# An issue order made in several passes, with a backward layout and estimates for partial and strided operations

## The chip, the cores and the metric

The kernel runs on one core of a Trainium2 chip. A core has five engines that work side by side, each through its own stream of instructions in the order of issue: TensorE (PE, with its weight loads shown apart as PEld), VectorE (DVE), ScalarE (ACT), GpSimd (POOL) and SyncE (SP), which here only issues DMAs. An instruction that waits for another engine holds up everything behind it on its own engine. The metric is the device time in microseconds (us) of one launch.

## What is computed

Two layers are applied to a prompt of 512 tokens and a sample of 256 tokens, with the same weights and 1024 channels: layer 0 is a bidirectional Mamba-2 mixer, layer 1 a bidirectional RWKV-7 mixer, each followed by a residual and a LayerNorm.

```python
alpha = (2.0 * DEPTH) ** 0.25            # DEPTH = 2
h = _mamba2_mixer(x, ...)                # layer 0
x = _layernorm(alpha * x + h, ln_g[0], ln_b[0])
h = _rwkv7_mixer(x, ...)                 # layer 1
x = _layernorm(alpha * x + h, ln_g[1], ln_b[1])
...
def step(s, inp):                        # RWKV-7, one token, once forwards and once backwards
    r_t, w_t, k_t, v_t, kk_t, a_t = inp
    sa = jnp.einsum('bhvk,bhk->bhv', s, -kk_t)
    s = (s * w_t[:, :, None, :] + sa[..., None] * (kk_t * a_t)[:, :, None, :]
         + v_t[..., None] * k_t[:, :, None, :])
    return s, jnp.einsum('bhvk,bhk->bhv', s, r_t)
...
y = (y - mu_y) * lax.rsqrt(var_y + R_GN_EPS) * ln_w + ln_b
out = (y + bonus) * g                    # then out @ w_out
```

All numbers are float32.

## The kernel before

**Arithmetic.** The 768 tokens of both sequences are handled together. A dense float32 product is three matmuls in a reduced float32 format: each operand is split into a high and a low part, and `mm3` (L140 to L142) adds high x high, high x low and low x high. Weights come in through `load_w`: a DMA (L121), a cast on ACT that makes the high part `whi` (L122), and a subtraction on DVE that makes the low part `wlo` (L123). The activations `xT` are loaded and split in the same manner (DMA L189, cast L135, subtraction L136).

**Stages.** First come the Mamba layer with its input projections, its chunked scan, its output projection and its LayerNorm. Then comes RWKV, in eight blocks `b` of 128 channels (two heads each). For a block, `rwkv_in` makes the projections r, k, v, g (dense matmuls, `pj`) and writes some of them to DRAM; the normalized key needs a row of norms that makes a trip through DRAM (`rows` L790, `rsd`, DMA `rb` L795) before DVE can form `k` (L796). `p1` works on six windows of 256 tokens: `p1_front` loads the block's streams again as `Wr` (DMA L853) and makes the decays (ACT L862 to L869); `p1_back` multiplies them on POOL into `G` (L888, L890) and takes matmuls of them (`ptd` L899). `rwkv_inverse` inverts the triangular matrices of all chunks: a long row of small DVE pairs (L949, L950), two transposes on DVE (L951, L953), and then the end of the inverse:

- PE multiplies the off-diagonal quarter (`pe`, L963) in two groups of 16 and 8 chunks,
- ACT writes each group back (L965, two instructions per group),
- ACT copies the diagonal quarters into `TD` (L968, L969; 32 partitions, a strided read; 16 chunks, "32x16x32", twice each, and 8 chunks, "32x8x32", twice each),
- PE multiplies again (`px`, L973), which needs all of L965, and L976 puts the result into `TD`.

The first `chain_step`s of the block need `px`; the copies of 8 chunks concern the sample's second half of chunks and are first read at step 4. `rwkv_final` normalizes the block's output `Y` per head: `rsqrt` on DVE by Newton steps (L102 to L107, `ngy`), a product on POOL (L1087), transposes on PE (`pf` L1091), ACT (L1097), POOL (L1100), DVE (L1101). In the program `p1(b+1)`, `rwkv_final(b)` and `rwkv_inverse(b+1)` follow the chain steps of block b. At the end stands the output projection with LayerNorm (L497, L512 to L526, `lnv` L522).

**The order.** The program text only lays out what is to be done. `arrange` (L1741) builds a `Program`: the graph of dependencies, and for each instruction an estimated duration (`estimate`, L1336). `schedule` (L1534) then is a list scheduler: it walks forward in an estimated time, and whenever an engine is free it takes the ready instruction with the best priority. The priority is the length of the longest path to the end (`tails`, L1516), in which every engine is taken to be free. A `Machine` (L1685) models what the scheduler believes of the engines: the clock of PE, modes of the PE array, DVE and POOL getting in each other's way, the DMA queue. For PE, four numbers (`Params`, L1245) decide when dense and small matmuls change places. The order that results is fixed for each engine; data waits come on top. One rule of `estimate` that the change touches (L1393): an ACT operation of N elements per partition is estimated at 51 + 0.8333 N ns, and 43 ns more without PSUM.

Of the kernel before, what the change touches and what calls it, by code (L numbers as in the profile page):

```python
# [58 lines left out]
class Trunk:  # L59
# [9 lines left out]
    def __init__(self, ctx, tc, d, y_p, y_s):  # L69
        self.ctx, self.tc, self.nc, self.d = ctx, tc, tc.nc, d  # L70
        self.out = (y_p, y_s)

        self.steps, self.gates, self.gate = {}, [], None
        self.cst = self.pool("cst", 1)
        self.bigx = ctx.enter_context(ExitStack())
        self.open_big(self.bigx, KB)
        self.pj = self.pool("pj", 1, PSUM, ctx=self.bigx, side="right")
        self.dr = self.pool("dr", 1, DRAM)
        self.ln_sm = self.pool("lnsm", 2)
        self.ident = self.cst.tile([P, P], F32, name="ident")  # L80
# [1155 lines left out]
NODE = "node"  # L1236
# [2 lines left out]
WARM = 2900  # L1239
SPAN = 3400  # L1240
TURN = 95.0
FULL = (128, 128)


class Params:  # L1245
    keep, pace, stay, spare = 4000.0, 1.6, 1000.0, 2.3


def size(ap, first=1):
    return math.prod(int(n) for _, n in ap.ap[first:])  # L1250
# [33 lines left out]
def space(t, name):  # L1284
    return str(t._space).endswith(name)


class Program:


    def __init__(self, nc, tc):
        self.ins = ins = list(nc.cur_bb.bb.instructions)
        n = len(ins)
        self.eng = [str(x.engine).split(".")[-1] for x in ins]
        self.pred = [set() for _ in ins]
        self.cost, self.dma, self.cols = [0.0] * n, [0.0] * n, [0.0] * n
        self.cells, self.kind = [()] * n, [1] * n
        self.mode, self.lock = [FULL] * n, [0.0] * n
        self.after, self.rationed = defaultdict(set), set()
        self.raw = set()  # L1300
        aps, self.acc = [], defaultdict(list)
        for i, x in enumerate(ins):
            io = [[a.bass_ap for a in l if getattr(a, "bass_ap", None) is not None] for l in (x.ins, x.outs)]
            aps.append(io)
            for b in io[0] + io[1]:
                if hasattr(b.tensor, "cap_key"):
                    self.acc[b.tensor.name].append(i)
            if io[0] or io[1]:
                self.estimate(i, x, *io)
        self.trace(nc, tc, aps)  # L1310
        self.classify()
# [24 lines left out]
    def estimate(self, i, x, src, dst):  # L1336
# [7 lines left out]
        if e == "PE":  # L1344
# [28 lines left out]
                self.kind[i] = 0  # L1373
            return
        N = max(size(a) for a in src + dst)
        ps = any(space(a.tensor, "PSUM") for a in src + dst if hasattr(a.tensor, "_space"))
        ptr = sum(1 for a in src if size(a) == 1 and N > 1)
        two = len(src) - ptr
        if e == "DVE":
            if op != "TensorScalarPtr":  # L1380
                c = (66 + N) / 0.96
                if op == "Reciprocal":
                    c = 70 + N * 6.4
            elif x.ins and two == 1 and not ps:
                c = 69 + N / 1.92 + 61 * ptr
            else:
                c = (66 + N) / 0.96 + 61 * ptr
            if getattr(x, "is_tensor_tensor_scan", False):
                c = 70 + 2.07 * N
            if not ps and N > 16:  # L1390
                self.lock[i] = c - 60
        elif e == "Activation":
            c = 51 + N * 0.8333 + (0 if ps else 43) + 93.5 * ptr + (93 if len(dst) > 1 else 0)  # L1393
        elif op == "Memset":
            c = 35 + 0.8333 * N
        elif op == "TensorScalarPtr":
            c = 130 + N * 0.83 + 90 * ptr
            self.lock[i] = c - 60
        elif two > 1:
            c = 160 + 1.6 * N if N < 200 else 190 + 1.75 * N  # L1400
            self.lock[i] = c - 60
        else:
            c = 130 + 0.9 * N
            self.lock[i] = c - 60
# [126 lines left out]
                    todo.append(j)  # L1531
        return tail

    def schedule(self, par=Params):  # L1534

        n, eng, pred, mode, kind = len(self.pred), self.eng, self.pred, self.mode, self.kind
        prio = [-v for v in self.tails()]  # L1540
        succ, asucc = [[] for _ in range(n)], defaultdict(list)
        for i, s in enumerate(pred):
            for j in s:
# [137 lines left out]
        del order[NODE]  # L1681
        return order


class Machine:  # L1685


    def __init__(self, p):
        self.p, self.free = p, defaultdict(float)
        self.mode, self.ring = FULL, 0.0  # L1690
        self.cell = [0.0] * 16
        self.work, self.held = defaultdict(float), {"DVE": 0.0, "Pool": 0.0}

    def run(self, i, t):

        p, e = self.p, self.p.eng[i]
        if e == NODE:
            return t
        if e == "PE":
            return self.matmul(i, t)  # L1700
        end = t + p.cost[i]
        if p.lock[i]:
            other = "Pool" if e == "DVE" else "DVE"
            end = max(end, self.held[other] + p.lock[i])
            self.held[e] = end
        self.free[e] = end
        if p.dma[i]:
            self.ring = max(self.ring, t + DMA_NS) + p.dma[i]
            end = self.ring
        return end  # L1710
# [73 lines left out]
```

## Time and profile before

| | |
|---|---|
| time before, median of 3 runs | 1726.08 us (1723.99, 1726.08, 1730.06) |
| the profiled execution's own time | 1718.15 us |
| its span | 1716.4 us |
| PE busy | 1546.6 us, 90% of the span, 15210 matmuls |
| DVE busy | 1362.4 us, 79%, 3041 instructions |
| ACT busy | 889.4 us, 52%, 1998 instructions |
| POOL busy | 758.4 us, 44%, 1026 instructions |
| mean granted clock of PE | 0.95 of full speed |

The profile comes from one execution. Its time is 1.75 us more than its span, and 7.93 us (0.46%) less than the median. "Busy" counts the time in which an engine executes; a busy PE may still run at a reduced clock, which the row PEclk gives in tenths of full speed. Rows of the timeline give the start, the duration, the engine and line, the output and inputs, and in brackets how long the engine was idle before and what ended this wait.

### The profile page before, as it was taken

Reading aid. Unit: us, or ns where it says so; the run is one execution under the profiler, and the core shown is the slowest. Engines: PE = TensorE matmul, PEld = TensorE weight load, DVE = VectorE, ACT = ScalarE, POOL = GpSimd, SP = SyncE. Lnnn points to the kernel's source line nnn. Section 1 sums busy time; section 2 is a strip of 40 time slices with the busy share of each in tenths; the row PEclk is TensorE's granted clock in tenths of the full one; section 3 lists DMA queues with packets and bytes.
Section 4 is the critical chain, followed back from the end, with each engine's and each line's share of the span. In section 5 each row is a group of like instructions: output and inputs, shape, how many; then the busy total and the mean of one; then the engine's idle time right before and its main releaser. Section 6 shows DMA issues by size and latency. Waiting matters only on the chain. (4 is left out here: it accounts for less than half of the span.)

```text
span 1716.4 us, 39466 instructions
## 1 busy us (share of the span) xinstructions
PE 1546.6 (90%) x15210; PEld 1302.3 (76%) x15210; DVE 1362.4 (79%) x3041; ACT 889.4 (52%) x1998; POOL 758.4 (44%) x1026
## 2 busy tenths in 40 slices
PE   7999999999999899998878989899898989878893
PEld 6887878888888799997667677677777767666783
DVE  5779988797897884678687878869797978969578
ACT  3344444545445442325556657485657657484432
POOL 1068356556565450021443626364554728274203
PEclk9999999999999899999988989889898989989996
DMA  5121211221211251603343243433434343444321
GB/s 162 38 62 32 69 56 38 62 81 56 69 44 56 66 169 60 201 38 114 111 133 116 83 125 86 123 102 109 132 99 130 88 119 91 126 144 123 116 62 74
DMA packets 150318, 161.42 MB, mean 94 GB/s; under 512 B 39633, under 2 KB 106929, under 8 KB 150129
## 3 DMA queue, kind: packets, MB, share of 16 engines
q1 hardware_dynamic: 150128, 158.89, 30.8%
q8 instruction: 120, 1.97, 0.5%
q14 instruction: 70, 0.57, 0.1%
HBM read 121.43 MB, written 40.55 MB: 94 GB/s over the span
## 5 line engine op out<-in xcount | busy, mean ns | idle before, releaser
L140 PE MATMUL pj<-xh,whi 128*128 128x256 f32 (+1 forms) x1056 | 385.0, 366 | 19.7 <-ACT whi L122 10.8
L142 PE MATMUL pj<-xh,wlo 128*128 128x256 f32 (+1 forms) x1056 | 381.5, 364 | 7.2 <-DVE wlo L123 7.2
L141 PE MATMUL pj<-xl,whi 128*128 128x256 f32 (+1 forms) x1056 | 381.7, 362 | 0.8 <-DVE xl L136 0.8
L140 PEld LDWEIGHTS pj<-xh,whi 128*128 128x128 f32 x1056 | 208.7, 198 | 53.9 <-ACT whi L122 12.0
L142 PEld LDWEIGHTS pj<-xh,wlo 128*128 128x128 f32 x1056 | 208.7, 198 | 35.8 <-DVE wlo L123 10.2
L141 PEld LDWEIGHTS pj<-xl,whi 128*128 128x128 f32 x1056 | 208.9, 198 | 26.1 <-DVE xl L136 1.6
L123 DVE TENSOR_TENSOR wlo<-wraw,whi 128x512 fp32r<-128x512 f32 x217 | 163.3, 756 | 76.4 <-ACT whi L122 70.8
L122 ACT CAST whi<-wraw 128x512 fp32r<-128x512 f32 x217 | 134.2, 620 | 126.4 <-PE pj L141 57.4
L414 POOL TENSOR_SCALAR G<-past,ddt,dt 128x128 f32<-128x128 f32 x192 | 131.1, 694 | 130.1 <-PE py L419 67.9
L140 PE MATMUL po<-whi,xh 128*128 128x256 f32 x528 | 154.1, 292 | 2.8 <-DVE acc L497 2.1
L141 PE MATMUL po<-wlo,xh 128*128 128x256 f32 x528 | 152.4, 289 | 0.7 <-DVE wlo L123 0.7
L142 PE MATMUL po<-whi,xl 128*128 128x256 f32 x528 | 152.4, 289 | 0.5 <-DVE xl L136 0.5
L234 DVE SCALAR_TENSOR_TENSOR conv<-conv,convw 128x770 f32<-128x770 f32 x128 | 140.5, 1099 | 0.5
L140 PE MATMUL pz<-whi,xh 128*128 128x256 f32 x384 | 113.4, 297 | 4.3 <-ACT vT L277 2.8
L378 POOL TENSOR_TENSOR xw<-xB,dtws 128x256 f32<-128x256 f32 x64 | 52.6, 826 | 138.5 <-ACT xB L366 122.8
L142 PE MATMUL pz<-whi,xl 128*128 128x256 f32 x384 | 110.8, 289 | 0.0
L141 PE MATMUL pz<-wlo,xh 128*128 128x256 f32 x384 | 109.9, 287 | 0.4 <-DVE wlo L123 0.4
L888 POOL TENSOR_TENSOR G<-EP,Wr 64x256 f32<-64x256 f32 x96 | 83.9, 875 | 57.1 <-DMA Wr<-ind 50.2
L1040 POOL TENSOR_TENSOR ZP<-SV,PC 64x128 f32<-64x128 f32 x128 | 64.9, 513 | 97.2 <-DVE SV L1052 84.5
L140 PEld LDWEIGHTS po<-whi,xh 128*128 128x128 f32 x528 | 101.2, 192 | 5.9 <-DVE acc L497 3.0
L141 PEld LDWEIGHTS po<-wlo,xh 128*128 128x128 f32 x528 | 101.2, 192 | 2.0 <-DVE wlo L123 1.2
L142 PEld LDWEIGHTS po<-whi,xl 128*128 128x128 f32 x528 | 101.2, 192 | 1.7 <-DVE xl L136 0.6
(272 smaller groups left out, 3942.8 us busy)
## 6 DMA issues: line engine op xcount, KB each, us to landing
wraw<-in_r_w_in SPq DMA_DIRECT2D x72, 256.0 KB, 2.7
Wr<-ind SPq DMA_DIRECT2D x48, 384.0 KB, 3.9
wraw<-in_m_w_xbc SPq DMA_DIRECT2D x64, 256.0 KB, 2.6
wraw<-in_m_w_z SPq DMA_DIRECT2D x32, 256.0 KB, 2.6
wraw<-in_m_w_out SPq DMA_DIRECT2D x32, 256.0 KB, 3.1
ydram<-yst SPq DMA_DIRECT2D x16, 384.0 KB, 2.4
yraw<-ydram SPq DMA_DIRECT2D x24, 256.0 KB, 5.9
ind<-k SPq DMA_DIRECT2D x32, 192.0 KB, 2.7
```

The costliest lines, as they stand in the source:

```text
L122: nc.scalar.copy(hi, raw)
L123: nc.vector.tensor_sub(lo, raw, hi.bitcast(F32))
L140: mm(ps, ah, bh, start=first, stop=False)
L141: mm(ps, ah, bl, start=False, stop=False)
L142: mm(ps, al, bh, start=False, stop=last)
L234: nc.vector.scalar_tensor_tensor(acc, u[:, t : t + n], w[:, b, t : t + 1], acc, op0=ALU.mult, op1=ALU.add)
L378: nc.gpsimd.tensor_tensor(hv(xw), hv(xB[c][:, 0:256]), bc(self.dtws[:, c, z, hs], 2, 64), op=ALU.mult)
L414: nc.gpsimd.tensor_scalar(G[:, h, :], self.past, self.ddt[:, c, i : i + 1], self.dt[:, c, 0, i : i + 1], op0=ALU.mult, op1=ALU.add)
L888: nc.gpsimd.tensor_tensor(G[hr, ps4, h, 0, :], EP[hr, :, 0:C], w4(tok(W[hr, h])), op=ALU.mult)
L1040: nc.gpsimd.tensor_tensor(ZP[HR[h], :, s, :], SV[HR[h], :, s, h, :], bc(pc[s][HR[h]], 2, C), op=ALU.mult)
```

## The change

No instruction is added to or removed from the computation; the arithmetic, the tiles and the matmuls' gates stay. What changes is how the order is made:

- `schedule` no longer makes one forward walk. For each of three sets of parameters it makes eight (`PASSES`): a forward walk with the priorities at hand, a replay of the order it gave (`timing`), and new priorities from `backward`. That one lays out the program from its end towards its start with engines that can only do one thing at a time, choosing by the ends that the replay gave. The order with the smallest planned end is kept.
- An instruction on ACT or DVE that touches only part of the partitions (32 or more) is taken to start `DRAIN` ns (122 and 90) after the one ahead of it; on ACT also the one behind it.
- An ACT operation with a stride of 16 or more elements in its last dimension, and more than 64 elements, is estimated at 1.9 ns per element rather than 0.8333.

```diff
+DRAIN = {"Activation": 122.0, "DVE": 90.0}
 class Params:
-    keep, pace, stay, spare = 4000.0, 1.6, 1000.0, 2.3
+    def __init__(self, keep, stay, pace, spare):
+        self.keep, self.stay, self.pace, self.spare = keep, stay, pace, spare
+
+PASSES = 8
+PARAMS = Params(4000, 1000, 1.6, 2.3), Params(6000, 1000, 1.6, 2.0), Params(5000, 2000, 1.6, 2.6)
...
+        rows = on_chip(dst[0])[:2] if hasattr(dst[0].tensor, "_space") and int(dst[0].ap[0][1]) > 1 else (0, 4)
+        if rows != (0, 4) and int(dst[0].ap[0][1]) >= 32:
+            self.part[i] = rows
...
         elif e == "Activation":
-            c = 51 + N * 0.8333 + (0 if ps else 43) + 93.5 * ptr + (93 if len(dst) > 1 else 0)
+            far = any(N > 64 and len(a.ap) > 1 and abs(int(a.ap[-1][0])) >= 16 for a in src + dst)
+            c = 51 + N * (1.9 if far else 0.8333) + (0 if ps else 43) + 93.5 * ptr + (93 if len(dst) > 1 else 0)
...
-    def schedule(self, par=Params):
+    def forward(self, par, prio):
...
-        prio = [-v for v in self.tails()]
...
+    def backward(self, end):
...
+        def push(j, t, by=1):
+            ready[j] = max(ready[j], t)
+            left[j] -= by
+            if not left[j]:
+                heapq.heappush(coming[eng[j]], (ready[j], -end[j], j))
...
+        for _ in range(n):
+            t, e = min((free[e] if heaps[e] else max(free[e], coming[e][0][0]), e) for e in names if heaps[e] or coming[e])
+            while coming[e] and coming[e][0][0] <= t:
+                heapq.heappush(heaps[e], heapq.heappop(coming[e])[1:])
+            i = heapq.heappop(heaps[e])[1]
+            if e != NODE:
+                free[e] = t = t + cost[i]
+            else:
+                t = ready[i]
+            tail[i] = t + (DMA_NS + self.dma[i] if self.dma[i] else 0)
+            for j in self.pred[i]:
+                push(j, tail[i] + self.lag(j, i))
+            for j in self.after.get(i, ()):
+                push(j, tail[i] - cost[j])
+        return tail
+
+    def timing(self, order):
...
+        while True:
+            best = min(((max(ready[q[0]], m.free[e]), e) for e, q in queue.items() if q and not left[q[0]]), default=None)
+            if best is None:
+                break
+            go(queue[best[1]].popleft(), best[0])
+        assert not any(queue.values())
+        return end
+
+    def schedule(self, par=None):
+        best = None
+        for p in [par] if par else PARAMS:
+            prio = [-v for v in self.tails()]
+            for _ in range(PASSES):
+                order = self.forward(p, prio)
+                end = self.timing(order)
+                if best is None or max(end) < best[0]:
+                    best = max(end), order
+                prio = [-v for v in self.backward(end)]
+        self.makespan = best[0]
+        return best[1]
...
 class Machine:
...
+        if e in DRAIN and (p.part[i] or e == "Activation" and self.part[e]):
+            t = max(t, self.free[e] + DRAIN[e])
         end = t + p.cost[i]
```

What this does to the order is shown at three places. In a row, the line is followed by the operation, its output and inputs with their numbers, and the shape.

The first is ACT at the end of the inverse of block 4. Before:

```order
L968 COPY TD_9300<-TC_9306 32x16x32
L969 COPY TD_9300<-TC_9306 32x16x32
L968 COPY TD_9300<-TC_9306 32x16x32
L969 COPY TD_9300<-TC_9306 32x16x32
L965 ACTIVATE TL_9307<-pe_16109 32x512 x2
L968 COPY TD_9300<-TC_9306 32x8x32
L969 COPY TD_9300<-TC_9306 32x8x32
L968 COPY TD_9300<-TC_9306 32x8x32
L969 COPY TD_9300<-TC_9306 32x8x32
L122 CAST whi_16225<-wraw_16224 128x512
L965 ACTIVATE TL_9307<-pe_16109 32x256 x2
```

Now:

```order
L1097 ACTIVATE o_16003<-pf_16000,rpar_9250 128x2x64 x2
L122 CAST whi_16225<-wraw_16224 128x512
L968 COPY TD_9300<-TC_9306 32x16x32
L969 COPY TD_9300<-TC_9306 32x16x32
L965 ACTIVATE TL_9307<-pe_16109 32x512 x2
L968 COPY TD_9300<-TC_9306 32x16x32
L969 COPY TD_9300<-TC_9306 32x16x32
L1097 ACTIVATE o_16016<-pf_16013,rpar_9250 128x2x64 x2
L965 ACTIVATE TL_9307<-pe_16109 32x256 x2
```

The first write-back (L965, 32x512) now stands behind two copies of 16 chunks instead of four, the second (32x256) behind the other two; the copies of 8 chunks stand behind the second write-back, and the cast of a weight (L122) ahead of all. Two instructions of block 3's `rwkv_final` (L1097) stand ahead of each write-back's copies or between. Blocks 0, 5, 6 and 7 read alike, with one L1097 pair in block 6 only. In blocks 1 to 3 the second write-back also stands behind the three ACT instructions L862 to L864 of `p1_front` and one or two copies of 8 chunks (in blocks 2 and 3 also behind L914 and one pair of L1097, in block 3 behind one L724).

The second is DVE at the same place: the last pairs of the inverse, with the Newton steps of block 3's `rwkv_final` (`ngy`) and the `k` of a later block. Before:

```order
L950 TENSOR_TENSOR tl_16043<-tl_16043,XN_9308 128x30
L107 SCALAR_TENSOR_TENSOR ngy_15986<-ngh_15987,ngy_15986 128x12
L951 STREAM_TRANSPOSE XN_9308<-tl_16043 128x1024
L953 STREAM_TRANSPOSE TC_9306<-tl_16043 128x1024
L796 SCALAR_TENSOR_TENSOR k_14857<-rb_15120,rpar_9250,k_14857 128x768
L105 TENSOR_TENSOR ngh_15987<-ngy_15986 128x12
L726 SCALAR_TENSOR_TENSOR g_15126<-pj0_15139,hmu_9253,g_15126 128x511
L106 SCALAR_TENSOR_TENSOR ngh_15987<-ngh_15987,gv_15979 128x12
L726 SCALAR_TENSOR_TENSOR g_15126<-pj0_15139,hmu_9253,g_15126 128x511
L107 SCALAR_TENSOR_TENSOR ngy_15986<-ngh_15987,ngy_15986 128x12
```

Now, where the next two rows are L951 and L953:

```order
L796 SCALAR_TENSOR_TENSOR k_14857<-rb_15120,rpar_9250,k_14857 128x768
L949 TENSOR_TENSOR XN_9308<-TL_9307,tl_16043 128x108
L105 TENSOR_TENSOR ngh_15987<-ngy_15986 128x12
L950 TENSOR_TENSOR tl_16043<-tl_16043,XN_9308 128x4x27
L106 SCALAR_TENSOR_TENSOR ngh_15987<-ngh_15987,gv_15979 128x12
L949 TENSOR_TENSOR XN_9308<-TL_9307,tl_16043 128x84
L107 SCALAR_TENSOR_TENSOR ngy_15986<-ngh_15987,ngy_15986 128x12
L950 TENSOR_TENSOR tl_16043<-tl_16043,XN_9308 128x3x28
L949 TENSOR_TENSOR XN_9308<-TL_9307,tl_16043 128x58
L950 TENSOR_TENSOR tl_16043<-tl_16043,XN_9308 128x2x29
L949 TENSOR_TENSOR XN_9308<-TL_9307,tl_16043 128x30
L950 TENSOR_TENSOR tl_16043<-tl_16043,XN_9308 128x30
```

The last Newton step (L107), which stood six rows behind the second transpose, now stands six rows ahead of the first, and `k` (L796) twelve rows ahead of the first transpose instead of right behind the second. Between L796 and the first transpose lie, block by block from 1 to 6, now 10, 13, 4 and 12 rows with `k` ahead (blocks 1 to 4), and in blocks 5 and 6 it stands 1 behind and 2 ahead; before it stood 1, 7 and 19 rows ahead in blocks 1, 2 and 6 and 2 to 5 rows behind in blocks 3 to 5.

The third is ACT at the start: six pieces of the activations (`xh`) and the first weight (`whi_88`). Before:

```order
L135 CAST xh_61<-xraw_93 128x768
L135 CAST xh_61<-xraw_97 128x768
L135 CAST xh_61<-xraw_101 128x768
L122 CAST whi_88<-wraw_87 128x512
L135 CAST xh_61<-xraw_105 128x768
L135 CAST xh_61<-xraw_115 128x768
L135 CAST xh_61<-xraw_119 128x768
```

Now:

```order
L135 CAST xh_61<-xraw_93 128x768
L135 CAST xh_61<-xraw_97 128x768
L135 CAST xh_61<-xraw_101 128x768
L135 CAST xh_61<-xraw_105 128x768
L135 CAST xh_61<-xraw_115 128x768
L135 CAST xh_61<-xraw_119 128x768
L122 CAST whi_88<-wraw_87 128x512
```

The first weight's cast stands behind all six pieces rather than behind three. SP issues the loads in the same changed order: six pieces, then the first weight.

In the closing LayerNorm, 48 DVE instructions stand between the last L1105 and the first L522 now, and 65 did before.

More of the change, by code (lines that the diff above doesn't have):

```diff
@@ L1298, in __init__ @@
         self.mode, self.lock = [FULL] * n, [0.0] * n
+        self.part = [None] * n
         self.after, self.rationed = defaultdict(set), set()
@@ L1682, in schedule @@
         return order
+    def backward(self, end):
+        n, eng = len(self.pred), self.eng
+        left, ready, tail = [0] * n, [0.0] * n, [0.0] * n
+        cost = list(self.cost)
+        for i in self.group:
+            cost[i] *= len(self.cells[i]) / 14
+        for s in chain(self.pred, self.after.values()):
+            for j in s:
+                left[j] += 1
+        names = (NODE, "PE", "DVE", "Activation", "Pool", "SP")
+        coming, heaps, free = {e: [] for e in names}, {e: [] for e in names}, dict.fromkeys(names, 0.0)
+        def push(j, t, by=1):
[3 more added lines that the diff above has]
+                heapq.heappush(coming[eng[j]], (ready[j], -end[j], j))
+        for i in range(n):
+            if not left[i]:
+                push(i, 0.0, 0)
+        for _ in range(n):
[13 more added lines that the diff above has]
+        return tail
@@ new lines, in timing, with go @@
+    def timing(self, order):
+        n, eng = len(self.pred), self.eng
+        m = Machine(self)
+        left, ready, end = [len(s) for s in self.pred], [0.0] * n, [0.0] * n
+        queue = {e: deque(l) for e, l in order.items()}
+        succ, asucc = [[] for _ in range(n)], defaultdict(list)
+        for i, s in enumerate(self.pred):
+            for j in s:
+                succ[j].append(i)
+        for i, s in self.after.items():
+            left[i] += len(s)
+            for j in s:
+                asucc[j].append(i)
+        def go(i, t):
+            end[i] = z = m.run(i, t)
+            todo = [(j, t) for j in asucc.get(i, ())]
+            todo += [(j, (t if eng[i] == eng[j] == "PE" else z + self.lag(i, j))) for j in succ[i]]
+            for j, x in todo:
+                ready[j] = max(ready[j], x)
+                left[j] -= 1
+                if eng[j] == NODE and not left[j]:
+                    go(j, ready[j])
+        for i in range(n):
+            if eng[i] == NODE and not left[i]:
+                go(i, 0.0)
+        while True:
[5 more added lines that the diff above has]
+        return end
@@ L1688, in __init__ @@
     def __init__(self, p):
-        self.p, self.free = p, defaultdict(float)
+        self.p, self.free, self.part = p, defaultdict(float), defaultdict(lambda: None)
         self.mode, self.ring = FULL, 0.0
@@ L1705, in run @@
             self.held[e] = end
-        self.free[e] = end
+        self.part[e], self.free[e] = p.part[i], end
         if p.dma[i]:
```

## The prediction

> **What bounds the kernel now.** I read the slices of the span first, then the table of stages.
>
> ```profile
> PE   7999999999999899998878989899898989878893
> PEclk9999999999999899999988989889898989989996
> ```
>
> PE is busy nine tenths or more until slice 19 and falls to eight or seven in every third or fourth slice behind it. There its granted clock falls too. So the first half has little to give, and the holes of the second half need to be found.
>
> ```profile
> 19.00:86.00 67.00, 61.57 (x378) 51.88 (x377) 45.93 (x66) 20.54 (x41) 4.05 (x8) 1.00 0.16 49
> 86.00:601.00 515.00, 494.32 (x3540) 423.58 (x3540) 430.67 (x837) 243.94 (x535) 295.19 (x372) 0.99 0.18 58
> 601.00:770.00 169.00, 168.79 (x1438) 164.80 (x1436) 115.66 (x307) 55.99 (x102) 32.36 (x41) 1.00 0.38 118
> 770.00:925.00 155.00, 126.59 (x973) 104.09 (x973) 119.02 (x253) 86.83 (x179) 46.80 (x61) 0.93 0.40 121
> 925.00:1612.00 687.00, 611.55 (x7956) 484.32 (x7956) 566.51 (x1313) 440.98 (x1054) 349.08 (x502) 0.92 0.39 112
> 1612.00:1716.00 104.00, 73.00 (x892) 64.73 (x892) 74.38 (x259) 30.84 (x77) 25.68 (x31) 0.84 0.22 68
> ```
>
> The columns are the stretch, its length, busy time of PE, PEld, DVE, ACT and POOL, the granted clock, the DMA share and GB/s. Mamba with its output (19 to 770) leaves PE idle for 26 us of 751. The stretch from 925 to 1612 holds seven RWKV blocks, from one `px` to the next (98 us each). PE is idle there for 75.5 us, 10.8 per block, at clock 0.92; no other engine is busier than DVE's 82%. So dependencies bound this stage, with PE close behind. The last stretch is the tail of block 7 and the closing LayerNorm.
>
> What stands in the holes, the timeline of block 4 shows:
>
> ```profile
> 1305.40 1.98 PE L963 MATMUL pe<-XN,TD 32*32 32x32 f32 x64 [0.44 <-DVE TC L953]
> 1305.47 1.08 ACT L968 COPY TD<-TC 32x512 f32<-32x512 f32 x1
> ...
> 1308.79 1.10 ACT L969 COPY TD<-TC 32x512 f32<-32x512 f32 x1
> 1309.90 1.19 ACT L965 ACTIVATE TL<-pe 32x512 f32<-32x512 f32 x2
> 1311.11 0.62 ACT L968 COPY TD<-TC 32x256 f32<-32x256 f32 x1
> ...
> 1313.67 0.62 ACT L122 CAST whi<-wraw 128x512 fp32r<-128x512 f32 x1
> 1314.31 0.76 ACT L965 ACTIVATE TL<-pe 32x256 f32<-32x256 f32 x2
> 1315.10 0.81 ACT L1097 ACTIVATE o<-pf,rpar 128x128 f32<-128x128 f32 x2
> 1315.13 2.92 PE L973 MATMUL px<-TC,TL 32*32 32x32 f32 x96 [2.04 <-ACT TL L965]
> ```
>
> `pe` is done at 1307.4, but ACT writes its result back only at 1309.90, behind four copies; `px` waits for ACT's second write-back and begins 9.73 us after `pe`. The chain of block 5 cannot start without `px`. The other blocks look the same, from the first to the last:
>
> ```profile
> 915.26 1.98 PE L963 MATMUL pe<-XN,TD 32*32 32x32 f32 x64 [1.28 <-DVE TC L953]
> 924.95 1.27 PE L973 MATMUL px<-TC,TL 32*32 32x32 f32 x38 [1.22 <-ACT TL L965]
> ...
> 1602.13 1.98 PE L963 MATMUL pe<-XN,TD 32*32 32x32 f32 x64
> 1612.08 1.10 PE L973 MATMUL px<-TC,TL 32*32 32x32 f32 x32 [2.24 <-ACT TL L965]
> ```
>
> From `pe` to `px` it is 9.69 and 9.95 us here, 78 us over the eight blocks.
>
> **1. The end of the inverse.** No instruction comes or goes. In block 4 the path from `pe` to `px` now holds four long copies (about 1.1 each, 4.4), the two write-backs (1.19 and 0.76) and no short copies (four of 0.62) and no cast (0.62): 6.4 us. An L1097 pair (0.81) between them makes 7.2. By the rows of the order, blocks 0, 5 and 7 come to 6.4, and 4 and 6 to 7.2. Block 1 carries L862 to L864 and one short copy as well. Such an ACT operation on 256 elements takes 0.42 (L869):
>
> ```profile
> 1301.16 0.42 ACT L869 ACTIVATE ld<-ld 128x256 f32<-128x256 f32 x1
> ```
>
> That gives 6.4 + 3 x 0.42 + 0.62 = 8.3. Block 2 has L914 (0.42) and an L1097 pair besides, 9.5; block 3 another short copy and an L724 (about 0.4), 10.5. The sum is 19.2 + 14.4 + 28.3 = 62 us, 16 less than now.
>
> Is the path worth its whole length? Two windows of ten us around it answer, the first in block 4, the second in block 3:
>
> ```profile
> 1310.00:1320.00 10.00, 7.59 (x143) 6.27 (x142) 3.91 (x5) 6.89 (x14) 3.94 (x5) 0.67 0.44 134
> 1210.00:1220.00 10.00, 7.59 (x137) 6.68 (x133) 2.65 (x5) 9.82 (x16) 1.48 (x1) 0.79 0.43 120
> ```
>
> PE is idle for 2.41 us of ten; in the rest it runs dense matmuls for later blocks, which must then be run elsewhere. If they find no other hole, only 24% of the 16 us is won, 4 us; if they all do, 16. The holes elsewhere (10.8 - 2.4 = 8.4 us per block) are larger than what is displaced, but lie where the order may not reach. No row is nearer to one end, so I take the middle: **-10** (-4 to -16).
>
> **2. `rwkv_final` and the next block's preparation on POOL.** POOL has a long wait at the same place. The table of waits (waiting instruction, releaser, total us, times, longest):
>
> ```profile
> POOL Y L1087 <- DVE ngy L107: 58.6, 6, 13.2
> POOL o L1100 <- ACT o L1097: 49.6, 11, 9.2
> POOL G L888 <- DMA Wr<-ind: 50.2, 7, 24.2
> DVE k L796 <- DMA rb<-rsd: 9.3, 4, 6.7
> ```
>
> In block 4 it reads:
>
> ```profile
> 1307.99 1.47 POOL L1087 TENSOR_TENSOR Y<-Y,ngy 128x768 f32<-128x768 f32 x1 [6.15 <-DVE ngy L107]
> 1309.54 1.24 SPq L853 DMA_DIRECT2D Wr<-ind  x2
> 1315.98 0.73 POOL L1100 TENSOR_TENSOR o<-o,bo 128x256 f32<-128x256 f32 x1 [6.51 <-ACT o L1097]
> 1316.66 0.68 POOL L888 TENSOR_TENSOR G<-EP,Wr 64x256 f32<-64x256 f32 x1
> ```
>
> L888, the first product of the next block's `p1_back`, stands in POOL's queue behind L1087 and L1100, and these behind the Newton steps and L1097. In the new order the last Newton step is ahead of the transposes and L1097 ahead of the write-back, so neither holds POOL any more. What then ends last is the load `Wr`: issued at 1309.54, and by the DMA table
>
> ```profile
> Wr<-ind SPq DMA_DIRECT2D x48, 384.0 KB, 3.9
> ```
>
> landed 3.9 us later, at 1313.4. L888 can start 3.2 us sooner, 25.6 over eight blocks. That is one end. The other is nothing, since POOL makes only 6% of the chain that ends last:
>
> ```profile
> PE 15%; DVE 10%; POOL 6%; issue 6%; ACT 5%; DMA 4%; SPq 1%; DVEq 0%; POOLq 0%; ACTq 0%
> ```
>
> I take a third, nearer to that small share: **-8** (0 to -25.6).
>
> **3. The start.** ACT now makes all six `xh` before the first weight's high part:
>
> ```profile
> 7.23 0.61 ACT L122 CAST whi<-wraw 128x512 fp32r<-128x512 f32 x1
> ...
> 10.57 0.84 ACT L135 CAST xh<-xraw 128x768 fp32r<-128x768 f32 x1 [0.16 <-DMA xraw<-in_xT]
> ...
> 7.90 0.79 PE L140 MATMUL pj<-xh,whi 128*128 128x512 f32 x1 [7.90 <-ACT whi L122]
> ```
>
> The sixth cast ends at 11.41; with 0.61 for the weight the first matmul comes at 12.1, 4.2 later. Part is made good: PE is idle for 5.4 us between 19 and 86, waiting for loads. **+2.5** (0 to +4.2).
>
> **4. Mamba.** PE is idle there for 26 us, the weights' waits are scattered, and instructions move both ways. **0** (-8 to +8): no more than a third of the idle time either way.
>
> **5. The tail.** The first ACT pass of the closing LayerNorm waits for DVE:
>
> ```profile
> 1685.56 0.41 DVE L512 BATCH_NORM_STATS2 lnst<-acc 128x6 f32<-128x256 f32 x1
> 1686.07 2.93 ACT L525 ACTIVATE acc<-acc,lnv,lny 128x512 f32<-128x512 f32 x4 [14.07 <-DVE lnv L522]
> ```
>
> Now 48 DVE instructions stand ahead of the first L522 instead of 65. At 0.4 us each (L512's duration) that would be 7 us earlier, but those moved behind still delay the later rows. **-3** (0 to -7).
>
> The rest (weights' loads on SP, DVE casts) lies under PE's dense work.
>
> **The sum**: -10 - 8 + 2.5 + 0 - 3 = -18.5. The profiled execution took 1718.15 us (span 1716.4 and 1.75 around it), which gives 1699.65. It was 7.9 below the median of the runs; from the median, 1726.08 - 18.5 = **1707.6 us**.
>
> **The rivals.**
>
> *`k` stalls DVE.* In blocks 1 to 4, `k` (L796) now stands 4 to 13 rows ahead of the transpose that `pe` waits for. DVE works in order: if the DMA `rb` is late, the last pairs of the inverse, the transposes, `pe` and `px` all wait behind `k`. The waits' row for it shows 9.3 us in four times, 6.7 at worst. With the worst in four blocks it is 26.8 us, and the sum is +8.3: **1734.4**. It decides from 18.5 / 4 = 4.6 us per block. Against it: `k` stood ahead in blocks 1, 2 and 6 before, and the mean of these waits is 2.3.
>
> *The clock falls further.* In the windows above the clock was 0.67 and 0.79 where small matmuls stand close together and dense ones are few; the new order leaves fewer dense ones between `pe` and `px`. From 925 to 1612 PE is busy for 611.55 us at 0.92; at 0.89 it would be 611.55 x (0.92 / 0.89 - 1) = 20.6 us more, and the sum +2.1: **1728.2**. From 0.893 the gain is gone. Against it: the same dense work only moves, and each hole closed raises the clock. The Trainium skill (TensorE: Matmul & The Clock Gate, in "What's actually happening") says that PE falls to half rate after an idle window of about 3.4 us; by that rule this rival could not occur, as the waits at these places get shorter. The row disagrees, for 0.67 stands where PE's longest wait was 2.04 us and PE was busy for 76%, so I leave the rival its chance.
>
> *Displaced work pays back and POOL's earlier start is worth nothing.* Then -4 + 0 + 2.5 - 3 = -4.5: **1721.6**. For it speaks that DVE, busy for 82%, and PE, for 89%, have little room.
>
> *All of it counts.* With 25.6 in the second term: -10 - 25.6 + 2.5 - 3 = -36: **1690**. For it speaks that L888 to `ptd` is where the next block's preparation starts.
>
> That the change does nothing is ruled out by the order: write-backs and Newton steps did move. That it moves only what doesn't count is the third rival.
>
> **How the numbers follow.** Forecast 0.52, `k` 0.08, clock 0.10, paid back 0.15, all of it 0.15. A measurement of this kernel tells about 0.3% (5.2 us) from no change, so faster means below 1720.9. Faster: forecast and all of it, and a third of the paid-back case (0.05), 0.72. Slower: `k`, and a third of the clock's case (0.03), 0.11. The same: the other 0.17. The range goes from 1682 (the fourth rival with the first term at its full 16 and the tail at -5) to 1728 (the clock's case) and leaves out `k` and some of what lies below.
>
> **What the profile after would show.** Right: `px` 6.4 to 7.2 us behind `pe` in blocks 0 and 4 to 7, no shorter in block 3; L1087 and L1100 no longer waiting for Newton steps and L1097; the period from `px` to `px` about 2 us under 98; the first matmul near 12. Wrong: periods as before with `px` early (the work was displaced); DVE waiting at `k` for `rb` for more than 4.6 us per block; a clock below 0.9 in the blocks; or a change in Mamba of more than 8 us, which I put at nothing.

## The result and the profile after

| | before | changed |
|---|---|---|
| median | 1728.07 us (1723.99 to 1731.98, 4 runs) | 1674.92 us (1673.38 to 1678.89, 4 runs) |
| ratio, 95% interval | | 0.9696 [0.9666, 0.9726] |
| profiled execution, span | 1718.15, 1716.4 us | 1673.38, 1671.6 us |
| PE, DVE busy | 1546.6, 1362.4 us | 1540.2, 1367.6 us |

The change takes 53 us off the median: the forecast direction, and nearly three times the forecast size of 18.5 us. The time lies below the forecast range (1682 to 1728 us). The profiled executions differ by 44.8 us; the one of before lies 9.9 us under its median, the one after 1.5 us under its own. What follows is accounted for between these two.

The slices and the head of the chain that ended last, of the changed kernel:

```profile
PE   7999999999999899998889989999898989888893
PEclk9999999999999999999989999999898989988897
...
PE 32%; DVE 11%; POOL 6%; DMA 4%; ACT 4%; issue 3%; SPq 0%; DVEq 0%; POOLq 0%; ACTq 0%
```

On the page PE's share of the chain rose from 15 to 32%, but these are not shares of the same stretch: the chain could be followed back only to 924 us before, and to 661 us now. Counted in the seven blocks alone, PE has 34% of the chain before and 49% now, and POOL 13% and 12%. So more often than before what ends last is PE itself and not a hand-over. The stages of the changed kernel, with the columns as in the prediction and the last two bounds laid at its own first and last `px`:

```profile
19.00:86.00 67.00, 66.61 (x415) 56.86 (x413) 47.81 (x71) 22.81 (x44) 4.08 (x8) 1.00 0.18 57
86.00:601.00 515.00, 505.15 (x3629) 433.49 (x3627) 440.18 (x859) 250.93 (x547) 312.45 (x386) 0.99 0.20 63
...
907.00:1564.00 657.00, 601.43 (x7984) 484.71 (x7984) 567.99 (x1312) 442.18 (x1059) 341.65 (x505) 0.94 0.40 118
1564.00:1672.00 108.00, 73.87 (x870) 64.92 (x864) 75.81 (x259) 32.86 (x77) 26.47 (x30) 0.84 0.21 65
```

In the seven blocks PE's idle time fell from 75.5 to 55.6 us, and nearly the same matmuls (7956 and 7984 in the two stretches) took 10 us less (611.55 to 601.43) at a granted clock of 0.94 instead of 0.92. From 86 to 601, in Mamba, the idle time fell from 20.7 to 9.9 us.

To cut the span at the same events, these rows serve. Of before, the row of the matmuls `pz` of Mamba (count, shortest/median/longest ns, first and last start) and the timeline's last cast `x67h`, ahead of the closing LayerNorm; then the same of the changed kernel, with its first and last `px`:

```profile
L140 PE MATMUL pz<-whi,xh x384: 277/281/471, 59.9 to 625.7; 128*128 128x256 f32 x192
```

```profile
1668.48 0.41 ACT L1104 CAST x67h<-o 128x256 fp32r<-128x256 f32 x1
```

```profile
L140 PE MATMUL pz<-whi,xh x384: 276/281/472, 57.6 to 611.9; 128*128 128x256 f32 x192
```

```profile
907.20 2.89 PE L973 MATMUL px<-TC,TL 32*32 32x32 f32 x96
...
1563.53 2.89 PE L973 MATMUL px<-TC,TL 32*32 32x32 f32 x96
...
1627.45 0.41 ACT L1104 CAST x67h<-o 128x256 fp32r<-128x256 f32 x1
```

| stretch | before | after | difference | forecast |
|---|---|---|---|---|
| start to the first `pz` | 59.9 | 57.6 | -2.3 | +2.5 |
| to the last `pz` (Mamba) | 565.8 | 554.3 | -11.5 | 0 |
| to the first `px` | 299.3 | 295.3 | -4.0 | in the next row |
| to the last `px` (seven blocks) | 687.1 | 656.3 | -30.8 | -18 with the row above |
| to the last `x67h` (chain of the last block) | 56.4 | 63.9 | +7.5 | 0 |
| to the end (LayerNorm) | 47.9 | 44.2 | -3.7 | -3 |

The end of block 4's inverse in the changed kernel, with what stands around it:

```profile
1265.69 1.02 DVE L796 SCALAR_TENSOR_TENSOR k<-rb,rpar,k 128x768 f32<-128x768 f32 x1 [0.72 <-DMA rb<-rsd]
...
1267.69 1.47 POOL L1087 TENSOR_TENSOR Y<-Y,ngy 128x768 f32<-128x768 f32 x1 [10.40 <-DVE ngy L107]
...
1269.22 0.44 PE L1091 MATMUL pf<-ident,Y 128*128 128x128 f32 x2 [2.55 <-POOL Y L1087]
...
1269.99 1.23 SPq L853 DMA_DIRECT2D Wr<-ind  x2
...
1272.43 2.01 PE L963 MATMUL pe<-XN,TD 32*32 32x32 f32 x64
1273.75 1.12 POOL L888 TENSOR_TENSOR G<-EP,Wr 64x256 f32<-64x256 f32 x1 [2.43 <-DMA Wr<-ind]
1274.49 1.19 ACT L965 ACTIVATE TL<-pe 32x512 f32<-32x512 f32 x2 [1.11 <-PE pe L963]
...
1278.79 0.76 ACT L965 ACTIVATE TL<-pe 32x256 f32<-32x256 f32 x2
```

The second write-back ends 7.1 us behind the start of `pe`, as the sum said (7.2), and `px` follows. POOL's L888 starts 1.3 us behind `pe` instead of 11.3, and it waits for the load `Wr`, as was said too. `Wr` is issued 2.4 us ahead of `pe`; before it was 4.1 us behind. It follows `k`, which now runs 6.7 us ahead of `pe`. PE has got a new wait, at `pf`. The waits of PE in the blocks, before and after (total us, times, longest):

```profile
PE px L973 <- ACT TL L965: 11.3, 7, 2.1
PE pe L963 <- DVE ngy L107: 11.2, 3, 7.1
...
PE pl L858 <- ACT ta L863: 4.4, 9, 1.0
PE pf L1091 <- POOL Y L1087: 4.0, 1, 4.0
```

```profile
PE pf L1091 <- POOL Y L1087: 15.1, 7, 3.4
...
PE pl L858 <- ACT ta L863: 5.9, 5, 2.0
...
PE px L973 <- ACT TL L965: 2.8, 3, 1.6
```

The waits at `px` and `pe` are gone for the most part, and `pf` took back 11 us.

One sign that the prediction named did not show. POOL's L1087 still waits for the Newton steps, for 59.1 us where it was 58.6:

```profile
POOL Y L1087 <- DVE ngy L107: 59.1, 7, 10.4
```

It only waits earlier: in block 4 it now starts 4.7 us ahead of `pe` instead of 2.6 behind. L1100's wait for L1097 fell from 49.6 to 30.2 us.

### The profile page after: what moved, and what is told of

It reads as the page before. It is cut to its first block, busy times and chain, and to the rows that moved or that the text cites. A ratio compares the mean times of both kernels' runs of the same rounds, so it can differ in the third digit from the quotient of the medians.

```text
span 1671.6 us, 39458 instructions
## 1 busy us (share of the span) xinstructions
PE 1540.2 (92%) x15210; PEld 1306.1 (78%) x15210; DVE 1367.6 (82%) x3041; ACT 889.6 (53%) x1998; POOL 759.9 (45%) x1026
## 4 chain that ended last, share of the span: by engine, by line
PE 32%; DVE 11%; POOL 6%; DMA 4%; ACT 4%; issue 3%; SPq 0%; DVEq 0%; POOLq 0%; ACTq 0%
PE pj L141 4%; PE pj L140 4%; PE pj L142 4%; PE py L1026 2%; PE po L142 2%; PE po L140 2%; PE po L141 2%; PE ptd L899 2%; POOL G L890 2%; POOL G L888 1%; PE pr L1004 1%; PE pS L1004 1%; DMA Wr<-ind 1%; PE pz L1004 1%; PE pbk L909 1%
## 5 line engine op out<-in xcount | busy, mean ns | idle before, releaser
L142 PE MATMUL pj<-xh,wlo 128*128 128x256 f32 (+1 forms) x1056 | 376.9, 358 | 1.1 <-DVE wlo L123 1.1
L141 PE MATMUL pj<-xl,whi 128*128 128x256 f32 (+1 forms) x1056 | 376.4, 357 | 0.6 <-DVE xl L136 0.6
L122 ACT CAST whi<-wraw 128x512 fp32r<-128x512 f32 x217 | 133.6, 619 | 145.6 <-PE pj L141 67.5
L414 POOL TENSOR_SCALAR G<-past,ddt,dt 128x128 f32<-128x128 f32 x192 | 137.6, 727 | 88.2 <-DVE ddt L320 60.4
L888 POOL TENSOR_TENSOR G<-EP,Wr 64x256 f32<-64x256 f32 x96 | 80.8, 842 | 67.7 <-DMA Wr<-ind 57.2
```

Of the source, the lines that this page charges most:

```text
L122: nc.scalar.copy(hi, raw)
L141: mm(ps, ah, bl, start=False, stop=False)
L142: mm(ps, al, bh, start=False, stop=last)
L414: nc.gpsimd.tensor_scalar(G[:, h, :], self.past, self.ddt[:, c, i : i + 1], self.dt[:, c, 0, i : i + 1], op0=ALU.mult, op1=ALU.add)
L888: nc.gpsimd.tensor_tensor(G[hr, ps4, h, 0, :], EP[hr, :, 0:C], w4(tok(W[hr, h])), op=ALU.mult)
```

## The experiments

Ratios are to the kernel before, measured beside each run; [low, high] is the 95% interval. Against the changed kernel a run is compared by the quotient of the two ratios.

**Which part of the change.** Four kernels are the changed one with other tables or with the old estimates.

```diff
# e3_passes_only: estimates of before
-            self.part[i] = rows
...
-            c = 51 + N * (1.9 if far else 0.8333) + ...
+            c = 51 + N * 0.8333 + ...
# e4_estimates_only
+PASSES = 1
+PARAMS = (Params(4000, 1000, 1.6, 2.3),)
# e7_sets_only
+PASSES = 1
# e8_longer
+PASSES = 18
+PARAMS = (Params(4000, 1000, 1.6, 2.3),)
```

> Eight passes with three sets of parameters, but the estimates of before (no drain, strided ACT copies priced as others). Theory A (the estimate of the strided copies moves the write-backs of the inverse ahead of them, which is what pays): most of the gain is gone, 1710 to 1728 us. Theory B (the passes make the gain, whatever the estimates): 1675 to 1690 us.

> The new estimates, but one forward walk with the first set of parameters and the path lengths as priorities, as before. Theory A: 1680 to 1700 us. Theory B: 1715 to 1735 us, no gain beyond the order's chance.

> The three sets of parameters and the new estimates, with one forward walk each and the path lengths as priorities: the backward layout never acts. If the choice among several orders makes the gain: 1680 to 1700 us. If the backward layout makes it: 1720 to 1740 us, about as the one walk with the first set.

> The first set of parameters alone, with 18 passes instead of 8, all else as in the changed kernel. If the backward layout makes the gain, no matter which set it begins from: 1663 to 1680 us. If the third set, from which the changed kernel's order came, holds part of it: 1685 to 1710 us.

| run | median | ratio |
|---|---|---|
| e4: estimates, one walk, first set | 1739.93 | 1.0095 [1.0068, 1.0123] |
| e7: estimates, one walk, three sets | 1712.88 | 0.9919 [0.9904, 0.9933] |
| e3: passes and sets, estimates of before | 1683.26 | 0.9781 [0.9748, 0.9814] |
| e8: estimates, 18 passes, first set | 1679.02 | 0.9727 [0.9709, 0.9746] |
| all (the changed kernel) | 1674.92 | 0.9696 [0.9666, 0.9726] |

The estimates by themselves made the kernel 1% slower, though in that run `px` follows `pe` after 8.2 us on average instead of 9.8. The sets, with one walk each, gain 0.8%, less than was expected if the choice made the gain and more than if it made none. The passes with the backward layout are most of it: without them 0.9919, with them 0.9696, and they gain nearly as much from the first set (0.9727). The passes also give 24 orders to choose from instead of 3, and no run separates this from the layout itself. With the passes the new estimates are worth 0.9% (0.9781 to 0.9696). So theory A, that the estimates carry the gain, falls. In e3 `px` follows `pe` after 9.6 us, hardly sooner than before (9.8), and the kernel is 2.2% faster all the same.

**Which stage.** Two kernels join the two orders: the order of one inside Mamba (instructions below `cut`), of the other inside RWKV.

```diff
+    for e in new:
+        a, b = [i for i in one[e] if i < cut], [i for i in two[e] if i >= cut]
+        shape = two[e]
+        ia, ib = iter(a), iter(b)
+        plan[e] = [next(ia) if i < cut else next(ib) for i in shape]
```

> The new order inside the Mamba layer, the order of before inside the RWKV layer. Theory A (all of the gain lies in the RWKV blocks, at the end of the inverse and in POOL's earlier start, and the earlier end of Mamba in the profile after is given back while weights and the first RWKV block are waited for): 1726 to 1731 us, no change from before. Theory B (the layout from the end backwards shortens every stage for itself): the 14 us by which the Mamba matmuls end earlier in the profile after show in the time, 1712 to 1716 us.

> The order of before inside the Mamba layer, the new one inside the RWKV layer. Theory A: 1675 to 1680 us, the whole gain of 53 us. Theory B: 1687 to 1691 us, the gain without Mamba's 14 us.

e1 took 1715.01 us, 0.9950 [0.9930, 0.9970]: Mamba's order, the start included, is worth 9 us alone, so theory A, which gave it nothing, falls. e2 took 1703.28 us, 0.9877 [0.9846, 0.9909], which lies above both its ranges. The two gains make 30 us and not 53. In the profile of e2 the seven blocks take 655.0 us from `px` to `px` (656.3 in the changed kernel, 687.1 before), so the gain inside the blocks comes from the RWKV order alone. From the last `pz` to the first `px`, where RWKV's first dense matmuls stand between Mamba's last in a pattern laid out for the other order, e1 takes 306.7 us and e2 303.1, against 299.3 before and 295.3 in the changed kernel: the seam costs in such a joint.

The profiles of the other runs agree on Mamba. From the first to the last `pz` every order that has Mamba from the passes takes 552 to 555 us (ten runs), and every other 565 to 570 (eight runs).

The profile of e1 also tells how far two executions of one order can lie apart. Its blocks, in the order of before, took 695.4 us, 8 more than in the profile before. A difference of about 1 us in the period of a block is thus no more than that.

**The first term: the path from `pe` to `px`.** e5 moves nothing but ACT at this place in the kernel before; e6 puts the old sequence back into the changed one (`wide` are the copies of 16 chunks, `thin` those of 8, `tl` the write-backs).

```diff
# e5_act_early, in the order of before
+        line[lo : hi + 1] = wide[:2] + tl[:2] + wide[2:] + tl[2:] + rest
# e6_act_late, in the changed order
+        line[:] = line[:lo] + wide + [i for i in line[lo:] if i not in wide and i not in thin]
+        hi = line.index(tl[2])
+        line[hi:hi] = thin
```

> The order of before, with one thing moved: at the end of every block's inverse ACT issues two of its copies of 16 chunks, the first write-back (L965), the other two, the second write-back, and all else behind (copies of 8 chunks, casts of weights). px should stand 6.4 to 7 us behind pe instead of 9.8. Theory A (the prediction's first term: a shorter path from pe to px is worth -4 to -16 us, -10 taken): 1712 to 1724 us beside a before of 1727. Theory B (where the path alone is shortened, px only comes earlier, and PE waits for something else behind it): within 4 us of before.

> The changed kernel, with one thing put back: ACT issues all four copies of 16 chunks ahead of the first write-back and the four of 8 chunks ahead of the second, as before the change. px then stands at least 10 us behind pe in every block. Theory A: 4 to 16 us slower than the changed kernel, 1679 to 1691 us. Theory B: within 4 us of it, 1671 to 1679 us.

e5: 1735.36 us, 1.0036 [1.0019, 1.0053], slower by 0.4%. `px` came 8.0 us behind `pe` on average, in four blocks 7.2 to 7.5, and PE's wait there, 11.3 us before, is gone. What took its place, in the waits of PE in the blocks of e5:

```profile
PE pl L858 <- ACT ta L863: 23.6, 12, 4.9
```

4.4 us have become 23.6. The timeline of its block 4 (where `pe` starts at 1322.30) shows why:

```profile
1329.71 2.89 PE L973 MATMUL px<-TC,TL 32*32 32x32 f32 x96
...
1337.61 0.47 ACT L862 ACTIVATE ld<-pl,w0a 128x256 f32<-128x256 f32 x1 [3.06 <-DVE KB L891]
1337.98 0.47 ACT L863 ACTIVATE ta<-pl,w0a 128x256 f32<-128x256 f32 x1
...
1338.50 0.58 PE L858 MATMUL pl<-lora,wuh 128*128 128x256 f32 x1 [3.54 <-ACT ta L863]
```

`pl`, of the next block's preparation, needs its PSUM bank back from L862 and L863, and these wait for DVE's L891 in the window ahead. L862 starts 15.3 us behind `pe`; in the profile before it is 14.4 us (1319.84). `px` is over two us earlier, and what PE needs next is not. The preparation was what ended last.

e6: 1685.29 us, 0.9758 [0.9743, 0.9773], 0.6% or 10.7 us slower than the changed kernel. By the two intervals this is 5 to 16 us. In the new order the early write-back is worth about what the forecast gave it (-10); in the old one it costs. The old sequence was put into an order laid out for the new one, so 10.7 us is an upper estimate.

**The second term: when POOL's L888 starts.** In the runs made up to here, the period of a block goes with this and not with `pe` to `px` (the table below: before, e1 to e8 and the changed kernel). e9 and e10 tell the scheduler where `rwkv_final` of a block is to stand beside the next inverse; `then` adds an edge between two instructions of one engine.

```diff
# e9_final_first, in the kernel before
+        then("DVE", at["ng", b], "DVE", at["flip", b + 1])
+        then("PE", at["pf", b, 1], "PE", at["pe", b + 1])
+        then("Activation", at["o", b, 0], "Activation", at["copy", b + 1])
# e10_final_late, in the changed kernel
+        then("Activation", at["copy", b + 1] - 1, "Activation", at["o", b, 0] - 1)
+        then("Pool", at["bonus", b, 0], "Pool", at["G", b + 2])
```

> The scheduler of before (one walk, old estimates, first set), told three things for every block: the last Newton step (L107) stands ahead of the transposes of the next block's inverse on DVE, the first two pairs of pf ahead of pe on PE, and the first pair of L1097 ahead of the diagonal copies on ACT. ACT's copies and write-backs stay as they were. Theory C (the period of a block is set by when POOL can start the following block's preparation, its first L888 behind pe, which the profile before shows at 8.7 us and the one after at 3.3): L888 comes at 3 to 5 us, the period falls from 98 to 94 us, 1695 to 1708 us in all. Theory A (pe to px counts by itself): no more than 8 us of gain, 1718 to 1728 us.

> The changed kernel's passes, sets and estimates, with one thing asked of them for every block up to the sixth: the first L1097 of a block stands behind the write-backs of the next block's inverse on ACT, and POOL's first L888 of the following block behind the first L1100. All else is free to be planned anew. Theory C: L888 comes 8 us or more behind pe again, the period goes back to 97 to 99 us, and 20 to 35 us of the gain are lost, 1695 to 1710 us. Theory A: the order of the write-backs stays good and no more than 8 us are lost, 1675 to 1683 us.

e9: 1733.17 us, 1.0050 [1.0032, 1.0069]. e10: 1676.67 us, 0.9721 [0.9702, 0.9741]. Both failed as tests, since neither moved L888 as meant. In e9 it stayed at 10.2 us behind `pe`: the first L1100 came early, but a second one now stood ahead of L888, which in four of seven blocks follows it without a wait, as in block 5 (`pe` at 1408.6):

```profile
1418.88 0.73 POOL L1100 TENSOR_TENSOR o<-o,bo 128x256 f32<-128x256 f32 x1 [9.93 <-ACT o L1097]
1419.56 0.68 POOL L888 TENSOR_TENSOR G<-EP,Wr 64x256 f32<-64x256 f32 x1
```

In the other three it waits for `Wr`. In e10 the edge held one of the two products of a window, and the passes put the other's ahead of L1100, at 4.8. So neither tells whether the place of `rwkv_final` holds L888. The profile before does: in blocks 3 to 5 L888 starts right behind L1100, as the prediction's rows of block 4 show, and in blocks 0 to 2 and 6 it waits for `Wr`, as in block 2 (`pe` at 1114.3):

```profile
1118.32 0.68 POOL L888 TENSOR_TENSOR G<-EP,Wr 64x256 f32<-64x256 f32 x1 [3.16 <-DMA Wr<-ind]
```

In the changed kernel it waits for `Wr` in blocks 0 to 5. `Wr` follows `k`, so the next runs have one demand on the place of `k`:

```diff
# e12_k_late, in the changed kernel: k behind the second transpose
+        then("DVE", at["pe", b] - 1, "DVE", at["k", b + 1])
# e13_k_first, in the kernel before, and e14_k_both, in the changed one: ahead of the 24th pair
+        then("DVE", at["k", b + 1], "DVE", at["pair", b, 24])
# e15_k_mid, in the kernel before, and e16_k_mid_both, in the changed one: ahead of the 29th
+        then("DVE", at["k", b + 1], "DVE", at["pair", b, 29])
```

> The changed kernel's passes, sets and estimates, with one thing asked of them: in every block, k (L796) of the next block stands behind the second transpose (L953) of the inverse on DVE. Theory D (k sets when the load Wr can start, Wr when POOL's L888 can, and that the period): k at pe or later, L888 at 8 to 11 us behind pe, period 97 to 99, 1695 to 1715 us. Theory E (the early L888 only goes along with an order that is good for other reasons): the passes find an order without it, 1672 to 1685 us.

> The scheduler of before (one walk, old estimates, first set), told one thing: k of the next block stands ahead of the 24th pair of the inverse on DVE, about twenty rows ahead of the transposes. Theory D: L888 at 2 to 6 us behind pe in every block, period 94 to 96, 1698 to 1715 us. Theory E: 1722 to 1735 us, as before, the wait having moved.

> The changed kernel's passes, sets and estimates, and k ahead of the 24th pair in every block as in the run before. Theory D: a little more than the change, 1665 to 1675 us, as blocks 0 and 5 gain too. Theory E: one order among others, 1672 to 1685 us.

> The scheduler of before (one walk, old estimates, first set), told that k of the next block stands ahead of the 29th pair of the inverse on DVE, which is 5 to 14 rows ahead of the transposes, as in the changed order. If k's place is enough by itself: period 94 to 96 us, 1698 to 1712 us. If it only pays where the rest of the order is laid out for it: 1720 to 1735 us, no gain.

> The changed kernel's passes, sets and estimates, with k ahead of the 29th pair in every block. If blocks 0 and 5 still have something to gain: 1663 to 1672 us. If it is one good order among others: 1673 to 1685 us.

The table has, from each run's timeline, means of the starts against the start of `pe` (`k` and L888 over blocks 0 to 5, `px` over all eight), the period over seven blocks, and the ratio. A period comes from one execution, a ratio from all; the profile before lies 9.9 us under its median, that of e5 5.9 over its own.

| run | `k` | L888 | `px` | period | ratio |
|---|---|---|---|---|---|
| before | -1.2 | +8.7 | +9.8 | 98.2 | 1 |
| e1 | -1.2 | +8.6 | +9.8 | 99.3 | 0.9950 |
| e4 | +0.2 | +9.0 | +8.2 | 100.3 | 1.0095 |
| e5 | -1.3 | +9.0 | +8.0 | 101.0 | 1.0036 |
| e7 | +0.3 | +9.3 | +8.0 | 97.9 | 0.9919 |
| e9 | -0.3 | +10.2 | +9.4 | 100.0 | 1.0050 |
| e13 | -9.1 | -0.4 | +9.6 | 99.5 | 1.0077 [1.0051, 1.0102] |
| e15 | -6.0 | +3.7 | +8.9 | 98.9 | 1.0024 [1.0007, 1.0041] |
| e12 | +1.0 | +10.3 | +8.1 | 96.9 | 0.9823 [0.9790, 0.9856] |
| e14 | -10.1 | -1.3 | +7.9 | 96.9 | 0.9858 [0.9832, 0.9885] |
| e2 | -4.9 | +3.7 | +8.3 | 93.6 | 0.9877 |
| e3 | -3.7 | +6.7 | +9.6 | 94.7 | 0.9781 |
| e6 | -5.0 | +3.5 | +10.5 | 95.8 | 0.9758 |
| e8 | -3.8 | +5.0 | +8.8 | 94.5 | 0.9727 |
| e10 | -4.7 | +4.8 | +7.4 | 94.7 | 0.9721 |
| changed | -5.2 | +3.3 | +8.6 | 93.8 | 0.9696 |
| e11 | -4.7 | +4.1 | +8.0 | 93.9 | 0.9697 |
| e16 | -5.9 | +2.5 | +9.3 | 92.5 | 0.9658 [0.9633, 0.9684] |

e12 (1693.48 us) is 1.3% or 22 us slower than the changed kernel, although the passes were free to plan around the late `k`. That lies between its two ranges. Its blocks take 22 us more (7 x 3.1). The DVE waits of its blocks, then those of the changed kernel, show one place:

```profile
DVE KB L885 <- DMA Wr<-ind: 26.7, 7, 6.2
```

```profile
DVE KB L885 <- DMA Wr<-ind: 7.5, 5, 4.6
```

DVE is not PE, though: of the 22 us, PE idles for 8.4 and is busy for 13.7 more, at a granted clock of 0.92 instead of 0.94.

And an early `k` is not enough. e15 puts it at the changed kernel's distance in the scheduler of before (1731.78 us): L888 comes at 3.7 us, and the period stays at 98.9. e13 (1739.06 us) and e14 (1700.13 us) put it some ten us ahead, and lose more than either theory allowed: e14 is 1.7% or 28 us slower than the changed kernel. Theory D, that L888's moment sets the period by itself, falls with e13 and e15. The profile before speaks against it too: there L888 came early in blocks 1, 2 and 6 (6.6, 4.1 and 2.4 us), and from `pe` to the next `pe` these took 102.1, 95.3 and 98.8 us, the others 95.8 to 99.1. Theory E's range is left by e12, but a demand on `k` the other way (e14) costs as much, so the 22 us may be the price of the demand and not of the late `k`. No run moved `k` alone in the changed order and left the rest of it in place. In e15 and e13 the waits have moved (PE's in e15, 4.0 us before, DVE's in e13, also 4.0):

```profile
PE pf L1091 <- POOL Y L1087: 19.3, 7, 3.7
```

```profile
DVE ld L865 <- ACT ld L864: 27.3, 11, 6.0
```

e16 (1669.53 us) is the fastest order measured, 0.4% under the changed kernel; the two intervals overlap, so this is no settled gain.

**The new wait at `pf`.**

```diff
# e11_pf_later, in the changed order: the first pair of pf behind five dense matmuls more
+        past = line[n + 1 : n + 6]
...
+            line[n - 1 : n + 6] = past + [last - 1, last]
```

> The changed kernel with the first pair of pf (L1091) moved behind the next five dense matmuls on PE in every block: the profile after shows PE waiting there for POOL's L1087 for 15.1 us in 7 blocks, with ready matmuls behind it. If that idle time lies on the way: 1 to 2 us per block less, 1660 to 1669 us. If the wait only moves, as in the run with ACT's early write-backs: 1672 to 1678 us, as the changed kernel.

1672.07 us, 0.9697 [0.9679, 0.9714], the changed kernel's ratio. PE's waits in its blocks:

```profile
PE pf L1091 <- POOL Y L1087: 9.6, 6, 2.2
...
PE pf L1091 <- ACT o L1097: 4.4, 7, 0.9
```

The wait fell by 5.5 us, 4.4 came up at a later pair of `pf`, and the time did not move.

## Why the prediction was wrong

The direction was right, and so was the main place, the blocks; the size was not, and two terms carry the miss.

**The second term, -8, was mis-sized.** The prediction took 25.6 us for the far end, and a third of it, "nearer to that small share", the 6% of POOL in the chain that ended last. Both steps failed. The 6% are of the whole span, of which the chain covers less than half; in the blocks POOL has 13%. And the far end took the issue of `Wr` as fixed, 4.1 us behind `pe`, so that L888 could gain no more than 3.2 us per block. But `k` moved, and `Wr` with it: L888 came 5.4 us sooner on average (8.7 to 3.3), 9.9 in block 4. The prediction took `k` ahead of the transposes for a risk alone (its first rival), while this was the step that let `Wr` start early. The waits at `rb` that the rival feared did not grow: 7.3 us in three times, against 9.3 in four before. It also read block 4 as the rule, where L1100 held L888; that was so in three blocks.

What an early L888 is worth stays open: the order with `k` held back is 22 us slower (e12), and an early `k` in the old order gains nothing (e15). What the profiles show is that the seven blocks and the stretch that leads to them became 34.8 us shorter where the first two terms gave 18; about 10.7 of it belongs to the first (e6).

**Mamba, 0, was mis-sized.** 11.5 us went there, beyond the 8 that were allowed, and e1 shows 9 us by the order of Mamba and the start alone. The step took it that moves both ways cancel. They did not: of the 26 us of PE's idle time from 19 us to the end of Mamba 12 were left, and every order from the passes has this gain. Which moves made it was not looked into.

**The first term, -10, has its size only in the new order.** e6 gives 10.7 us there, and in the old order the same move loses 6 (e5), where what PE needs next isn't early too. The prediction asked whether displaced matmuls would find a hole, and not what stands next in PE's queue behind `px`. By block the path came out at 6.7 to 7.7 us in blocks 0 and 4 to 7 (6.4 to 7.2 were worked out), 9.3, 10.9 and 12.7 in blocks 1 to 3 (8.3, 9.5 and 10.5): 9 us less in all, where 16 were worked out. That the middle of a wide range came close to e6 is in part luck.

**The start, +2.5, was wrong in sign.** The first matmul came at 11.54 us (12.1 was forecast), but from 19 to 86 PE was idle for 0.4 us instead of 5.4, and `pz` began 2.3 us sooner. The whole delay was made good, and more.

**The tail, -3, held for the LayerNorm (-3.7)**; the chain of the last block became 7.5 us longer, which no term had. No run looked into that.

Of the rivals, "all of it counts" (1690) came nearest, but with nothing for Mamba. The clock did not fall, it rose from 0.92 to 0.94 in the blocks. A smaller slip in the first reading, on which no term hangs: PE falls to eight or seven tenths in 14 of the 22 slices from slice 19 on, and in slice 14 already.

What stays open: why the period is 94 us and not 98 cannot be put down to one move. Three changes were tried one at a time on the old order or its scheduler (e5, e9, e15), and each lost 0.2 to 0.5%; two were taken back in the new order (e6, e12), and each cost. That what a move is worth depends on the rest of the order is shown by e5 and e6, where the same ACT instructions were moved by hand. That the moves need each other is not, since no run put two of them together into the old order.

## What to carry to other kernels

In this kernel, whose two busiest engines are busy for 80 to 90% of the span, a stall that was removed by itself was passed to a later instruction in the same queue (e5, e11). Before pricing such a stall, look at what the next instruction waits for, and whether that comes early too. Look also at what the order moves further up the chain of waits, as `k` here, before taking a start as fixed. Time the new order as a whole; a single move that loses in the old order may pay in the new one. Passes with a backward layout, in which engines are busy, made 2.2% here beyond what the choice of parameters gave.

## What was not expected of the chip

The matmuls of the seven blocks were busy for 10 us less at a granted clock of 0.94 instead of 0.92: a third of the blocks' gain of 30.8 us. This goes with the order, as the same stretch of e1 (blocks in the order of before) and of e2 (blocks in the changed order) shows:

```profile
916.00:1611.00 695.00, 621.04 (x7956) 493.31 (x7956) 569.96 (x1312) 442.46 (x1054) 346.19 (x504) 0.90 0.39 111
```

```profile
934.00:1589.00 655.00, 599.76 (x7965) 482.30 (x7964) 573.12 (x1313) 444.02 (x1058) 341.47 (x505) 0.94 0.41 118
```

It is 0.90 and 0.92 in the old order and 0.94 twice in the new one, so the clock's part of the gain is 10 to 21 us in these four profiles, and two executions of one order differ by 9.5 us. That smaller holes are the cause is not shown: e9 has 85.3 us of idle time in its blocks and e12 64.0, both at 0.92, and e16 58.5 at 0.96, where the changed kernel has 55.6 at 0.94. And e11, in which the wait at `pf` was partly filled, with a mean clock of 0.959, took the same time as the changed kernel (0.956).
